# Second pair of blocks: the output gate's columns move into the joint Strassen projection, and the value projection moves from the front of attention into the filler

## The chip, the cores and the metric

The kernel runs on one core of a Trainium2 chip. TensorE multiplies (it writes PSUM only), VectorE, ScalarE and GpSimd (POOL) do the rest, SyncE and the queues of ScalarE and GpSimd issue DMAs. The metric is the device time of one execution, in microseconds (us), as the median of several runs; lower is better.

## The reference

One layer of a hybrid decoder on 2048 prompt positions and 32 sample positions (8 sequences of 4), model width 1024, in float32:

```
h = rmsnorm(x, n1);  z = h @ w_in          # 1024 x 4864
hq, hf, hi, hg, sq, sk, sv, ga, gb = split(z)   # 512 512 512 512 512 128 128 1024 1024
f = lb + (1 - lb) * sigmoid(hf)
o = hgrn_recurrence(hq, log f, 1 - f, hi)  # 4 heads of 128; hi are the values
y_a = (rmsnorm(o) * silu(hg)) @ w_up_a     # hg is the output gate
q, k, v = rotary(sq), rotary(sk), sv       # 8 query heads, 2 key/value heads of 64
y_b = sliding_window_attention(q, k, v, window 128, sinks) @ w_up_b
x = x + (sigmoid(ga) * y_a + sigmoid(gb) * y_b) @ w_o
x = x + square(relu(rmsnorm(x, n2) @ w_ff1)) @ w_ff2;  y = rmsnorm(x, nf)
```

The sample positions attend to a cache of 128 keys and start from a given recurrent state.

## The kernel before, in words

**Precision.** Every large product is made of three matmuls: each operand is split into a high part (a cast on ScalarE) and a low part (a subtraction on VectorE), and high x high, high x low and low x high are summed in PSUM. `unit_rows` (through `unit`, L138, and `split_out`, L257 and L258) loads a block of weights by SyncE's queue and splits it; a block takes three of twelve weight tiles (raw, high, low) of tag "w", and raw is free after the split. So 1024 rows by 128 columns are 24 matmuls per run of up to 512 tokens.

**Blocks and pairs.** The prompt is cut into four blocks of 512 tokens; the last one also carries the 32 sample tokens (544 tokens, run as two segments of 288 and 256). Blocks 0 and 1 are the first pair, blocks 2 and 3 the second. The loop `for bi in range(nblk)` does projections, attention, recurrence, the two merge gates and the output projection of a block. After it come the two feed-forward layers by pairs, with Strassen's scheme (seven products for eight).

**The second pair's joint projection.** With the flag `zs` (second pair) the even block first projects its own attention columns (`colN512(C_SQ ...)`, `colN(C_SQ + 512 ...)`) and sends q, k, v to DRAM (`zqk`). Then it runs one Strassen stage (`strassen_T`) over both blocks' 1056 tokens, cut into four quarters of 528 tokens by the two halves of the model width, for NZ = 20 column tiles: the recurrence's query (HH = 4 tiles) and the merge gates gb and ga (8 each). Column tiles go by twos (`Wpair`), tokens by two chunks of 264 (`chunks_of`), so there are 10 x 2 units. A `Unit` makes seven products (`prod`, L264 to L266) of 12 matmuls; VectorE adds the partial results in PSUM (L329, L342, L359, L372), ScalarE copies (L327). `z_fin` finishes a quarter: it writes tanh(x/2) for the merge gates (L861) or plain values for the query to the DRAM tensor `zd`, from which both blocks of the pair load later (`kmaj(zd[sb], ...)`).

**Front of attention.** In block 2, q, k, v come back from DRAM (L921) into a buffer that the stage's operand A22 occupied, then the recurrence's query is loaded into `qW` (L922), and `colN512(C_HI ...)` projects the values `vN` (L191 to L193, 96 matmuls). In block 3 the attention columns are projected directly (L892, L896), and the value projection (120 matmuls: four prompt tiles and one of 32 sample rows) runs between the steps of the sample's attention: `smp_scores`, `smp_turn` and `smp_values` hang on it as hooks (`smp_at`).

**Attention.** `tc.manual_schedule` keeps TensorE's instructions of this part in program order; elsewhere the framework's scheduler places every engine's instructions, and each engine then runs its own list in order. A tile c of 128 tokens has four steps: `swa_turn` T (rotation on POOL, L933 to L936, then transposes of q and k, L939, L942), `swa_scores` S (L1061, then softmax on VectorE and ScalarE), `swa_probs` P (transposes, L1094, masked products L1097 and L1099 on VectorE) and `swa_values` V (L1108). Between them `fill(n)` issues n x segments matmuls of the filler, a list of generators (`fills`): the forget gate, four heads of `col_steps(C_HF, ...)` (L684, finished by `ev_f`, L703 to L705), and then head 0 of the output gate, whose result is held in PSUM (`hg_held`). The order and the n are written by hand:

```
for f, c in ((T_, 0), (fill, 6), (S_, 0), (T_, 1), (fill, 12), (S_, 1), (T_, 2), (fill, 24), (P_, 0), (fill, 16), (V_, 0), (S_, 2), (T_, 3), (fill, 10), (P_, 1),
             (fill, 10), (V_, 1), (S_, 3), (fill, 10), (P_, 2), (fill, 8), (V_, 2), (fill, 16), (P_, 3), (fill, 8), (V_, 3)):
```

That is 120 steps (120 matmuls in block 2, 240 in block 3).

**Recurrence.** `hgrn_levels` runs seven levels (1 to 64) for two groups of 256 tokens, and two for the sample, as generators that take turns. A level is small matmuls (`lv`, L771), multiplications on VectorE (L776, L777, L779) and copies of results (L785, L788, L795). Level 0 is the only one that reads the decay `fW`; afterwards the output gate is written over it. So `ev_g` (L718 to L720: tanh and copy on ScalarE, multiplication on VectorE) may write head 0 only after round 1, and heads 1 to 3 are projected (`colT(C_HG, ...)`, L165 to L167) at rounds 3, 4 and 6 (`hg_at`). At rounds 3 and 5 the gb gates are loaded into `pb` (L1147). Then come `lx` (L805), the output o (L1193), the key transposes, the state update u, and `hgrn_tail`, which multiplies the normed output by the gate in `fW`. `split_out` splits it for the product with w_up_a.

**Merge gates.** `gate(C_GB, ...)` multiplies attention's output by w_up_b (`ybb`), whose weights `ub` are loaded ahead (r_ubb), and then `gate(C_GA, ...)` the recurrence's output by w_up_a.

Of the kernel before, what the change touches and what calls it, by code (L numbers as in the profile page):

```python
# [16 lines left out]
P = 128  # L17
# [21 lines left out]
def F(ap):  # L39
    return ap.bitcast(F32)  # L40
# [3 lines left out]
def tile_hybrid_step(  # L44
# [381 lines left out]
    NZ = HH + 2 * KD  # L426
# [205 lines left out]
    for bi in range(nblk):  # L632
# [193 lines left out]
        if zs and not odd:  # L826
# [29 lines left out]
            with tc.tile_pool(name=f"zp{sb}", bufs=1, reuse_waits="tile") as zp:  # L856
                def z_fin(u, blk, x, ps=None):
                    o, nh = int(blk[1]) - 1, int(blk[2]) - 1
                    zi = 2 * u.n + nh
                    if zi >= HH:  # L860
                        nc.scalar.activation(x, x if ps is None else ps, AF.Tanh, scale=0.5)  # L861
# [6 lines left out]
                def z_src(n, kh):  # L868
                    zi = 2 * n
                    c0 = C_HQ + zi * P if zi < HH else (C_GB + (zi - HH) * P if zi < HH + KD else C_GA + (zi - HH - KD) * P)  # L870
# [16 lines left out]
        if smp and zs:  # L887
            nc.gpsimd.dma_start(qS, zd[sb][0:HH * P, z0:z0 + NS].rearrange("(h p) t -> p h t", p=P))
# [5 lines left out]
        def ev_skv(ps, kind, c, nr):  # L894
            ti = c if kind == "p" else ncb
            nc.scalar.activation(qkv[0:nr, ti, 512:768], ps, AF.Copy, scale=1.0 if bi else rs0[:, 0, c:c + 1])  # L896

# [21 lines left out]
        else:  # L919
            for c in range(ncb):  # L920
                nc.gpsimd.dma_start(qkv[:, c, :], zqk[sb][c * P:(c + 1) * P, :])  # L921
            nc.gpsimd.dma_start(qW, kmaj(zd[sb], 0, HH, z0 + ns, bt))  # L922
            colN512(C_HI, f"hi{B}", ev_v)
# [188 lines left out]
        fills = [col_steps(C_HF, h, f"hf{B}{h}", ev_f) for h in range(HH)] + [col_steps(C_HG, 0, f"hg{B}0", None, hg_held)]  # L1112

        def fill(n):
            while n and fills:
                if next(fills[0], fills) is fills:
                    fills.pop(0)
                else:
                    n -= 1

        T_, S_, P_, V_ = swa_turn, swa_scores, swa_probs, swa_values
        for f, c in ((T_, 0), (fill, 6), (S_, 0), (T_, 1), (fill, 12), (S_, 1), (T_, 2), (fill, 24), (P_, 0), (fill, 16), (V_, 0), (S_, 2), (T_, 3), (fill, 10), (P_, 1),
# [627 lines left out]
```

## Time and profile before

| | us |
|---|---|
| median of 3 runs | 2817.21 (2811.98 to 2823.4) |
| span of the profiled execution | 2810.0 |
| joint Strassen stage of the second pair | 758 to 965 |
| block 2: attention from its first turned query / first gate-b matmul | 986.6 / 1072.9 |
| block 3: end of its key/value projection / first turned prompt query / first gate-b matmul | 1236.1 / 1272.9 / 1366.2 |

The profile is one execution. A row of a group gives the line of the code, the engine, what is written from what, and the count, then the busy time and the mean of one. In the view by stage each engine's busy time stands beside its number of instructions, and PEclk is the share of full clock that TensorE was granted. [...] Rows of the timeline give start and duration. A DMA's row on its issuing queue is the issue, not the transfer.

### The profile page before, as it was taken

Reading aid. Unit: us, or ns where it says so; the run is one execution under the profiler, and the core shown is the slowest. Engines: PE = TensorE matmul, PEld = TensorE weight load, DVE = VectorE, ACT = ScalarE, POOL = GpSimd, SP = SyncE. Lnnn points to the kernel's source line nnn. Section 1 sums busy time; section 2 is a strip of 40 time slices with the busy share of each in tenths; the row PEclk is TensorE's granted clock in tenths of the full one; section 3 lists DMA queues with packets and bytes.
Section 4 is the critical chain, followed back from the end, with each engine's and each line's share of the span. In section 5 each row is a group of like instructions: output and inputs, shape, how many; then the busy total and the mean of one; then the engine's idle time right before and its main releaser. Section 6 shows DMA issues by size and latency. Waiting matters only on the chain.

```text
span 2810.0 us, 50089 instructions
## 1 busy us (share of the span) xinstructions
PE 2730.1 (97%) x20053; PEld 2403.9 (86%) x20053; DVE 1791.2 (64%) x2905; ACT 1110.0 (40%) x2070; POOL 490.9 (17%) x782
## 2 busy tenths in 40 slices
PE   8999999999999999899999999999999999999998
PEld 7778888788899977677898888878888999999998
DVE  5675746746774385637667777765567777654556
ACT  4542445423344353335334333434344233343332
POOL 1100211002300102320231221220012343320001
PEclk9999999999999999999999999999999999999999
DMA  5237662377743424652365544796566444485553
GB/s 190 75 103 237 208 198 76 97 242 256 251 126 115 144 76 149 219 160 67 105 210 184 181 145 150 265 317 222 190 200 215 147 161 135 155 291 184 189 187 119
DMA packets 344481, 487.60 MB, mean 174 GB/s; under 512 B 23432, under 2 KB 220824, under 8 KB 344248
## 3 DMA queue, kind: packets, MB, share of 16 engines
q1 hardware_dynamic: 289112, 329.10, 37.5%
q0 software_dynamic: 42880, 140.22, 13.8%
q10 hardware_dynamic: 12256, 15.08, 1.5%
q8 instruction: 157, 2.57, 0.4%
q14 instruction: 76, 0.62, 0.1%
HBM read 353.64 MB, written 130.68 MB: 172 GB/s over the span
## 4 chain that ended last, share of the span: by engine, by line
PE 78%; DMA 6%; DVE 6%; issue 5%; ACT 2%; POOL 2%; SPq 0%; POOLq 0%; DVEq 0%; ACTq 0%
PE f L1581 6%; PE f L1582 6%; PE f L1580 6%; PE fB_f L264 4%; PE fB_f L266 3%; PE fB_f L265 3%; PE fD_f L264 2%; PE fD_f L266 2%; PE fD_f L265 2%; PE ps_hfb L684 2%; PE fB_z L264 1%; PE fB_z L266 1%; PE fB_z L265 1%; PE wob L1390 1%; PE gab L166 1%
## 5 line engine op out<-in xcount | busy, mean ns | idle before, releaser
L1582 PE MATMUL f<-f2S,lw2T 128*128 128x264 f32 (+1 forms) x576 | 184.4, 320 | 2.0 <-DVE lw2T L152 2.0
L1580 PE MATMUL f<-f2S,hw2T 128*128 128x264 f32 (+1 forms) x576 | 184.5, 320 | 1.6 <-ACT hw2T L151 1.6
L1581 PE MATMUL f<-f2S,hw2T 128*128 128x264 f32 (+1 forms) x576 | 184.0, 319 | 0.0
L264 PE MATMUL fB_f<-S,w1T_f 128*128 128x264 f32 (+1 forms) x384 | 123.2, 322 | 3.1 <-ACT c_f L327 2.2
L152 DVE TENSOR_TENSOR lw2T<-lw2T,hw2T 128x1024 fp32r<-128x1024 f32 x64 | 78.2, 1224 | 69.7 <-ACT hw2T L151 68.8
L265 PE MATMUL fB_f<-S,w1T_f 128*128 128x264 f32 (+1 forms) x384 | 122.5, 319 | 0.0
L1580 PE MATMUL f<-f2A,h_w2B 128*128 128x264 f32 (+1 forms) x384 | 122.4, 319 | 0.0
L1581 PE MATMUL f<-f2A,h_w2B 128*128 128x264 f32 (+1 forms) x384 | 122.3, 319 | 0.0
L1582 PE MATMUL f<-f2A,l_w2B 128*128 128x264 f32 (+1 forms) x384 | 122.3, 318 | 0.0
L266 PE MATMUL fB_f<-S,w1T_f 128*128 128x264 f32 (+1 forms) x384 | 122.0, 320 | 0.0
L151 ACT CAST hw2T<-lw2T 128x1024 fp32r<-128x1024 f32 x64 | 67.2, 1051 | 137.2 <-DMA lw2T<-w_T 137.2
L1582 PEld LDWEIGHTS f<-f2S,lw2T 128*128 128x128 f32 x576 | 108.4, 188 | 10.4 <-DVE lw2T L152 2.9
L1580 PEld LDWEIGHTS f<-f2S,hw2T 128*128 128x128 f32 x576 | 108.8, 189 | 9.9 <-ACT hw2T L151 2.4
L1388 PE MATMUL wob<-m_b,h_wob 128*128 128x512 f32 (+2 forms) x320 | 113.1, 353 | 3.2 <-ACT h_wob L257 3.2
L1390 PE MATMUL wob<-m_b,l_wob 128*128 128x512 f32 (+2 forms) x320 | 112.4, 353 | 3.0 <-DVE l_wob L258 2.8
L1581 PEld LDWEIGHTS f<-f2S,hw2T 128*128 128x128 f32 x576 | 108.8, 189 | 7.6
L1389 PE MATMUL wob<-m_b,h_wob 128*128 128x512 f32 (+2 forms) x320 | 112.5, 352 | 0.0
L152 DVE TENSOR_TENSOR f2S<-f2S 128x1024 fp32r<-128x1024 f32 (+1 forms) x64 | 78.9, 1240 | 41.3 <-ACT f2S L151 40.9
L257 ACT CAST w1T_f<-w1r_f 128x512 fp32r<-128x512 f32 x128 | 77.1, 619 | 69.7 <-DVE w1r_f L300 29.7
L258 DVE TENSOR_TENSOR w1T_f<-w1r_f,w1T_f 128x512 fp32r<-128x512 f32 x128 | 87.4, 688 | 26.0 <-ACT w1T_f L257 25.7
L1507 POOL DMA_DIRECT2D u_A<-c_f x106 | 57.4, 541 | 236.1 <-DVE c_f L1491 225.1
L1507 POOL DMA_DIRECT2D u_S<-s_f x144 | 77.7, 541 | 109.0 <-DVE s_f L1502 92.4
(845 smaller groups left out, 9256.8 us busy)
## 6 DMA issues: line engine op xcount, KB each, us to landing
w1r_f<-w_ff SPq DMA_DIRECT2D x64, 512.0 KB
lw2T<-w_T SPq DMA_DIRECT2D x64, 512.0 KB
rw2B<-w_ff SPq DMA_DIRECT2D x48, 512.0 KB
f2S<-u_S SPq DMA_DIRECT2D x32, 528.0 KB
ws<-w_ff SPq DMA_DIRECT2D x32, 512.0 KB
r_wob<-w_o SPq DMA_DIRECT2D x32, 512.0 KB
f2S<-u_S SPq DMA_DIRECT2D x32, 512.0 KB
u_S<-s_f POOLq DMA_DIRECT2D x96, 132.0 KB, 2.3
```

The costliest lines, as they stand in the source:

```text
L152: pin(nc.vector.tensor_tensor(lo, F(lo), F(hi), ALU.subtract), on)
L258: pin(nc.vector.tensor_tensor(dl, src, F(dh), ALU.subtract), on)
L264: nc.tensor.matmul(ps, wh, ah, start=(first and k == 0), stop=False, skip_group_check=not first)
L265: nc.tensor.matmul(ps, wh, al, start=False, stop=False, skip_group_check=not first)
L266: nc.tensor.matmul(ps, wl, ah, start=False, stop=(last and k == 3), skip_group_check=not first)
L1388: nc.tensor.matmul(p, wh, ah, start=(k == 0), stop=False)
L1389: nc.tensor.matmul(p, wh, al, start=False, stop=False)
L1390: nc.tensor.matmul(p, wl, ah, start=False, stop=(k == KD - 1))
L1507: nc.gpsimd.dma_start(us[o][u.n // 4][u.n % 4 * P:(u.n % 4 + 1) * P, u.t0:u.t0 + u.ln], y_)
L1580: nc.tensor.matmul(ps, wh, ah, start=first, stop=False, skip_group_check=cont)
L1581: nc.tensor.matmul(ps, wh, al, start=False, stop=False, skip_group_check=cont)
L1582: nc.tensor.matmul(ps, wl, ah, start=False, stop=lastk, skip_group_check=cont)
```

## The change

Only the second pair changes.

- The output gate's four column tiles join the Strassen stage behind the query's: NZ goes from 20 to 24, 12 column pairs and 24 units. `z_fin` writes (1 + tanh(x/2)) x for them: tanh on ScalarE (into `carry` where x itself is not in PSUM), scalar_tensor_tensor on VectorE, the store on POOL's queue.
- The gate is no longer projected in the recurrence. `z_rows` loads it from DRAM into `fW` (and `fS`) at round 1 by POOL's queue. The norm weight, which `ev_g` multiplied in, is applied where the output is split.
- The value projection no longer stands in front of attention. It becomes a generator, `row_steps`, last in the filler: two token tiles first, then one at a time, with all four weight blocks kept.
- What the hand-written order does not use is issued by `fill(10000)` behind the levels in the program (the second pair only).
- The order of block 2 begins with 16 fill steps ahead of T_0 and has 112 in all; the order of block 3 takes in the sample's attention, also with 112 steps, where a step of the value projection counts two.
- Both blocks' query loads (`z_q`) come at one place, behind the load of q, k, v.

```diff
-    NZ = HH + 2 * KD
+    ZG, ZB, ZA = HH, 2 * HH, 2 * HH + KD
+    NZ = 2 * HH + 2 * KD
...
+        def row_steps(c0, name, fn):
+
+            us = []
+            for grp in [tiles[0:2]] + [[t] for t in tiles[2:]]:
+                ps = [mm_ps(f"ps_{name}_{t[3]}") for t in grp]
+                for i in range(KD // 2):
+                    if len(us) <= i:
+                        us.append(unit_rows(w_in, 2 * i, 2, c0, 512, f"{name}{i}"))
+                    uh, ul = us[i]
+                    for p, (kind, r0, nr, c) in zip(ps, grp):
+                        for kk in range(2):
+                            k = 2 * i + kk
+                            lh, ll = (x[:, r0:r0 + nr] for x in h_acts[k])
+                            for m, (a, w) in enumerate(((lh, uh), (lh, ul), (ll, uh))):
+                                nc.tensor.matmul(p[0:nr], a, w[:, kk, :], start=(k == 0 and m == 0), stop=(k == KD - 1 and m == 2))
+                                if k == KD - 1 and m == 2:
+                                    fn(p[0:nr], kind, c, nr)
+                                yield len(segs)
...
-                    if zi >= HH:
-                        nc.scalar.activation(x, x if ps is None else ps, AF.Tanh, scale=0.5)
-                    elif ps is not None:
-                        nc.scalar.copy(x, ps)
-                    q = nc.scalar if zi >= HH else nc.gpsimd
+                    src = x if ps is None else ps
+                    if zi < ZG:
+                        if ps is not None:
+                            nc.scalar.copy(x, ps)
+                    else:
+                        tg = carry[:, u.t0:u.t0 + u.ln] if ps is None and zi < ZB else x
+                        nc.scalar.activation(tg, src, AF.Tanh, scale=0.5)
+                        if zi < ZB:
+                            nc.vector.scalar_tensor_tensor(x, tg, 1.0, src, ALU.add, ALU.mult)
+                    q = nc.scalar if zi >= ZB else nc.gpsimd
...
-            nc.gpsimd.dma_start(qW, kmaj(zd[sb], 0, HH, z0 + ns, bt))
-            colN512(C_HI, f"hi{B}", ev_v)
+        if zs:
+            z_q()
...
-        if zs and odd:
-            nc.gpsimd.dma_start(qW, kmaj(zd[sb], 0, HH, z0 + ns, bt))
-            smp_at = {0: lambda: [smp_scores(kv) for kv in range(NKV)], 2: lambda: [smp_turn(kv) for kv in range(NKV)], 3: smp_values} if smp else {}
-            colN512(C_HI, f"hi{B}", ev_v, lambda i, ul: smp_at[i]() if i in smp_at else None)
...
-        fills = [col_steps(C_HF, h, f"hf{B}{h}", ev_f) for h in range(HH)] + [col_steps(C_HG, 0, f"hg{B}0", None, hg_held)]
+        fills = [col_steps(C_HF, h, f"hf{B}{h}", ev_f) for h in range(HH)]
+        fills += [row_steps(C_HI, f"hi{B}", ev_v)] if zs else [col_steps(C_HG, 0, f"hg{B}0", None, hg_held)]
...
+        elif not odd:
+            seq = ((fill, 16), (T_, 0), (fill, 6), (S_, 0), (T_, 1), (fill, 10), (S_, 1), (T_, 2), (fill, 20), (P_, 0), (fill, 10), (V_, 0), (S_, 2), (T_, 3), (fill, 8), (P_, 1),
+                   (fill, 8), (V_, 1), (S_, 3), (fill, 8), (P_, 2), (fill, 8), (V_, 2), (fill, 10), (P_, 3), (fill, 8), (V_, 3))
+        else:
+            seq = ((fill, 10), (q_scores, 0), (fill, 8), (T_, 0), (fill, 4), (S_, 0), (T_, 1), (q_turn, 0), (fill, 8), (S_, 1), (T_, 2), (q_values, 0), (fill, 18), (P_, 0), (fill, 10), (V_, 0),
+                   (S_, 2), (T_, 3), (fill, 8), (P_, 1), (fill, 8), (V_, 1), (S_, 3), (fill, 8), (P_, 2), (fill, 8), (V_, 2), (fill, 12), (P_, 3), (fill, 10), (V_, 3))
...
+                if rnd == 1:
+                    z_rows(fW, ZG, ns, bt)
+                    if smp:
+                        z_rows(fS, ZG, 0, NS)
...
+        fill(10000)
...
+                if zs:
+                    nc.scalar.activation(oa[:, 0, h, t0:t0 + n], gx[:, h, 0:n], AF.Copy, scale=hn5[:, h:h + 1])
+                    nc.vector.scalar_tensor_tensor(oa[:, 1, h, t0:t0 + n], gx[:, h, 0:n], hn5[:, h:h + 1], F(oa[:, 0, h, t0:t0 + n]), ALU.mult, ALU.subtract)
```

More of the change, by code (lines that the diff above doesn't have):

```diff
@@ L1117, in fill, with q_scores @@
                     fills.pop(0)
                 else:
[L1119 to L1123 removed]
+                    n -= m or 1
+        def q_scores(_):
+            for kv in range(NKV):
+                smp_scores(kv)
@@ L1124, in tile_hybrid_step @@
+        for f, c in seq:
             f(c * len(segs) if f is fill else c)
-        fill(1000)
+        if not zs:
+            fill(10000)
         pe_order.__exit__(None, None, None)
@@ L1155, in tile_hybrid_step @@
             rnd += 1
+        fill(10000)
         def hgrn_out(ops, nr, name):
```

39 lines of the change are left out of this document (26 added, 13 removed).

## The prediction

> **What bounds the kernel now.** I read the page first, for the engine that sets the end.
>
> ```profile
> PE 2730.1 (97%) x20053; PEld 2403.9 (86%) x20053; DVE 1791.2 (64%) x2905; ACT 1110.0 (40%) x2070; POOL 490.9 (17%) x782
> ...
> PE 78%; DMA 6%; DVE 6%; issue 5%; ACT 2%; POOL 2%; SPq 0%; POOLq 0%; DVEq 0%; ACTq 0%
> ```
>
> TensorE is busy 97% of the span and 78% of the chain that ended last. A change pays here by taking matmuls away or by filling the few places where TensorE stands still. The second view is the busy time by stage. I cut it at the second pair's joint projection, then for block 2 at the first turned query (T_0), at the first recurrence matmuls and at the first gate-b matmul; the last three rows cut block 3 likewise, from the end of its key/value projection.
>
> ```profile
> core 0: us, PE busy (x) PEld busy (x) DVE busy (x) ACT busy (x) POOL busy (x), PEclk, DMA share, GB/s
> 758.00:965.00 207.00, 206.86 (x1685) 205.06 (x1684) 112.09 (x200) 91.62 (x193) 11.68 (x21) 1.00 0.42 133
> 965.00:986.60 21.60, 21.60 (x95) 17.46 (x94) 4.24 (x4) 6.12 (x8) 10.82 (x20) 1.00 0.59 195
> 986.60:1026.40 39.80, 39.80 (x288) 30.55 (x286) 30.84 (x63) 24.74 (x87) 1.28 (x4) 1.00 0.20 54
> 1026.40:1072.90 46.50, 40.65 (x889) 29.85 (x888) 34.74 (x77) 17.83 (x43) 4.78 (x6) 0.96 0.41 117
> 1236.00:1272.90 36.90, 36.61 (x212) 28.38 (x210) 10.41 (x22) 13.50 (x30) 2.79 (x5) 1.00 0.41 116
> 1272.90:1327.50 54.60, 52.82 (x471) 45.72 (x470) 41.63 (x98) 31.09 (x115) 2.47 (x4) 1.00 0.20 51
> 1327.50:1366.20 38.70, 32.27 (x920) 30.24 (x918) 29.27 (x75) 14.80 (x39) 8.71 (x10) 0.91 0.43 123
> ```
>
> The joint projection is solid TensorE work. The value projection in front of attention (row two, and most of row five) is solid too, with VectorE nearly idle beside it. The recurrences (rows four and seven) are where TensorE stands: 5.85 us and 6.43 us, and their clocks of 0.96 and 0.91 lose up to 4% of 46.5 us (1.9) and 9% of 38.7 us (3.5) more. So the old idle time that a better filler could take is at most 17.7 us.
>
> **Matmuls that come and go.** For the direct gate projection I read starts in the timeline of TensorE: 24 matmuls of 512 columns in block 2, then 24 of 288 and 24 of 256 in block 3.
>
> ```profile
> 1050.76 0.50 PE L165 MATMUL ps_hgb<-hT,h_hgb 128*128 128x512 f32 x1
> ...
> 1056.54 0.34 PE L771 MATMUL lv_b2g<-W_b 128*32 128x16 f32 x19
> ...
> 1347.87 0.40 PE L165 MATMUL ps_hgb<-hT_b,h_hgb 128*128 128x288 f32 x1
> ...
> 1351.17 0.28 PE L165 MATMUL ps_hgb<-hT_b,h_hgb 128*128 128x256 f32 x1
> ...
> 1354.11 0.49 PE L771 MATMUL lv_b3g<-W_b 128*32 128x16 f32 x35
> ```
>
> From start to start one costs 5.78/24 = 0.241 us at 512 columns, 3.30/24 = 0.138 at 288 and 2.94/24 = 0.123 at 256. Four heads of 24 go away: 96 x 0.241 = 23.1 us in block 2 and 96 x (0.138 + 0.123) = 25.0 us in block 3. The Strassen stage ran 20 units (10 column pairs, two token chunks), 1685 matmuls in 207.0 us, 0.1229 us each. Two more pairs are 4 units of 84: 336 x 0.1229 = 41.3 us. Matmuls alone: 41.3 - 48.1 = **-6.8 us**. The seven-for-eight trade of Strassen is mostly eaten by 264-column matmuls that cost more per column.
>
> [...]
>
> The value projection keeps its matmuls (96 in block 2, 120 in block 3). Only their place changes.
>
> **Strassen stage, other engines.** VectorE's 112.09 us over 20 units is 5.6 us per 10.3 us unit; a gate unit adds four scalar_tensor_tensor and ScalarE four tanh. The nearest groups of that stage:
>
> ```profile
> L359 DVE TENSOR_TENSOR c_z<-fD_z,c_z 128x264 f32<-128x264 f32 x20 | 8.6, 430 | 19.8 <-ACT c_z L327 19.7
> L861 ACT ACTIVATE c_z<-c_z 128x264 f32<-128x264 f32 x43 | 18.2, 424 | 30.1 <-DVE c_z L359 12.4 <-DVE c_z L372 9.3 <-DVE c_z L329 4.2
> ```
>
> Four times 0.43 makes 7.3 us of VectorE per unit, under TensorE's 10.3. What is new is a wait: VectorE's multiply waits for ScalarE's tanh, and behind it stand the PSUM additions that free banks for TensorE. One such wait is about a tanh long, 0.42 us, and there are 16. If none shows it is 0, if half show 3 us. I take **+1**, since TensorE lost only 0.14 us in the whole stage. The gate stores go out on POOL's queue, idle here (11.68 of 207 us). The reload of the gates waits on that queue until level 0 of the recurrence has read the decay it overwrites; behind it stand the gate-b loads, which are first read at the first gate-b product, and the gates' own first reader is the first output tile. The rest of the recurrence covers both, so nothing is booked; without that cover it would be one load, about the 6 us that the q, k, v load below takes to its first use.
>
> **Front of attention, block 2.** The value projection covered the return of q, k, v from DRAM and the rotation on POOL:
>
> ```profile
> 964.04 2.12 POOL L921 DMA_DIRECT2D qkv_b<-zqk  x4 [2.87 <-PE fB_z L266]
> 970.14 1.25 POOL L933 TENSOR_TENSOR r_b2c<-qkv_b,rot 128x80 f32<-128x80 f32 x1 [3.97 <-ACT h_hfb L257]
> 971.35 0.35 POOL L934 TENSOR_TENSOR r_b2c<-qkv_b,rot 128x80 f32<-128x80 f32 x1
> 971.64 1.06 POOL L967 MEMSET qbd<- 128x1152 f32 x1
> ...
> 973.27 0.53 POOL L936 TENSOR_TENSOR qkv_b<-qkv_b,r_b2c 128x160 f32<-128x160 f32 x1
> ```
>
> The load is issued at 964.04, because its slot is freed by the last Strassen unit, and the first rotated tile is there at 973.80, 8.8 us after that stage ends at 965.05. TensorE's order is written by hand, so T_0 waits for it and everything behind T_0 too. The new cover is 16 forget-gate matmuls, 16 x 0.241 = 3.9 us. TensorE stands 4.9 us. After the last idle stretch of that length the granted clock fell:
>
> ```profile
> 1061.00:1071.00 10.00, 6.92 (x81) 5.17 (x81) 7.16 (x16) 5.36 (x14) 0.00 (x0) 0.83 0.05 16
> ```
>
> 17% of 10 us is 1.7 us more. I take **+6.6**. The unknown is the 6.1 us from issue to first use, which other loads shared; I allow half of it, 3.1 us, either way. Upper bound 9.7. Lower bound +1: 4.9 less 3.1 and less the MEMSET's 1.06 is 0.8, too short to move the clock.
>
> The first POOL operation took 1.25 us and its twin 0.35, beside a VectorE subtraction:
>
> ```profile
> 969.95 1.23 DVE L258 TENSOR_TENSOR l_hfb<-r_hfb,h_hfb 128x1024 fp32r<-128x1024 f32 x1 [4.26 <-PE ps_hib L192]
> ```
>
> This speaks against the change: the rotation is now on the path while weights are split beside it. [...]
>
> **Thinner fill in attention.** From T_0 on block 2 had 120 fill matmuls and now has 96; block 3 had 240 short ones, now 192 short and 16 long, two steps counted for each long one. Between the transposes of probabilities and the value product (P to V) the fill must cover VectorE:
>
> ```profile
> 1003.08 0.48 PE L684 MATMUL ps_hfb<-hT,h_hfb 128*128 128x512 f32 x1
> ...
> 1006.15 1.28 DVE L1099 TENSOR_TENSOR pc_b2c<-pT_b2c,pc_b2c 128x512 f32<-128x512 f32 x2
> ```
>
> The transposes end at 1003.08, the products are there at 1007.43: 4.35 us. The fill there goes from 16 to 10, 2.4 us, so 1.9 us open. The three later tiles go from 10, 8, 8 to 8 each and I give them 0.5 us each: 3.5 us per block, **+7** for both. Bounds 3 and 12.
>
> In block 3 the sample's softmax now has 24 short fills and one tile's scores with two turns to cover it, instead of 60 long matmuls:
>
> ```profile
> 1236.87 1.09 PE L964 MATMUL kcT<-ident,kc 128*128 128x128 f32 x8 [0.29 <-ACT SV_b L940]
> ...
> 1244.82 2.16 PE L987 MATMUL sps<-kcT,qbd 64*128 64x128 f32 x18
> ...
> 1248.38 0.30 PE L988 MATMUL sps<-kt_smp,qs 64*128 64x32 f32 x2
> ...
> 1259.74 0.30 DVE L1005 TENSOR_SCALAR ss<-ss,sms 128x160 f32<-128x160 f32 x1
> ...
> 1272.86 0.65 PE L939 MATMUL qT_b3c<-ident,qkv_b 128*128 128x128 f32 x4
> ...
> 1282.81 0.66 PE L939 MATMUL qT_b3c<-ident,qkv_b 128*128 128x128 f32 x4
> ```
>
> From the last score at 1248.38 to the weights at 1260.04 it took 11.7 us, but it had time. From T_0 to T_2 are 9.95 us with 36 fills (36 x 0.13 = 4.7), so one tile's scores with two turns take about 3.0, and the new cover is 24 x 0.13 + 3.0 = 6.1 us. I take **+1**, bounds 0 and 5.6.
>
> **Recurrence.** What stood idle in block 2 was the gate-b weights, in block 3 the gate held in PSUM, which may not overwrite the decay before level 0 has read it:
>
> ```profile
> ACT h_ubb L257 <- DMA r_ubb<-w_up_b: 8.9, 1, 8.9
> DVE l_ubb L258 <- ACT h_ubb L257: 6.0, 1, 6.0
> ...
> ACT W_b L719 <- DVE W_b L777: 4.4, 1, 4.4
> ```
>
> In block 2 a weight cast blocked ScalarE's and VectorE's queues, and with them the levels, so TensorE ran dry. Value rows have neither constraint: they write their own tile, leave PSUM with one copy, and can be placed from the first level on. Left for the recurrence are 80 of 96 in block 2 (72 gate matmuls before) and 104 of 120 long ones in block 3 (144 short before). I take 8 of block 3's 9.9 us back, and 4 of block 2's 7.8, because value weights hold eight of the twelve weight tiles meanwhile and a late weight can stall the same queues. **-12**, bounds -17.7 and -4.
>
> **The sum.** -6.8 + 1 + 6.6 + 7 + 1 - 12 = -3.2 us. On the profiled span of 2810.0 this is 2806.8. The median of the runs, 2817.21, lies 7.2 above that span, so I expect 2814.0. All low ends make -6.8 + 0 + 1 + 3 + 0 - 17.7 = -20.5 (2796.7); all high ends -6.8 + 3 + 9.7 + 12 + 5.6 - 4 = +19.5 (2836.7).
>
> **Rivals.** *Faster: the filler takes all old idle time.* For it: both causes named above go away with the gate. Then T_0 at 1, thin fill at 7, sample at 1, no tanh waits and the full 17.7: -15.5 us, 2801.7. Against it: the twelve weight tiles. Chance 0.26.
>
> *Slower: attention becomes bound by the chain through VectorE.* T_0 to gate b would last as long as now (86.3 us in block 2, 93.3 in block 3) whatever is filled. Block 2 then gains only its earlier T_0, 21.6 - 8.8 - 1.7 = 11.1 us. In block 3 only the transposes (2.0 us from 1236.0), the scores (1244.82 to 1248.68, 3.9) and 36 short fills (4.7) stand before T_0: 10.6 us instead of 36.9, 26.3 gained, but the sample's 10.41 us of VectorE move into the stretch: 15.9. Together 27.0 against 41.3 + 1: +15.3 us, 2832.5. It decides if VectorE's load there, 10.41 + 41.63 + 29.27 = 81.3 us, cannot be packed into about 100 us. For it: 41.63 of 54.6 us now. Against: twelve gate multiplications leave VectorE. Chance 0.08.
>
> *The value rows do not fill.* They are written after the level loop; if the scheduler leaves them there, 184 x 0.241 = 44.3 us run behind the levels. With half of it uncovered: 41.3 + 1 - 11.1 - 26.3 + 22.2 = +27.1 us, 2844.3. Against it: the gate matmuls of now are cut into pieces of 24 and fewer between levels (the rows from 1050.76 to 1056.54 are one). Chance 0.04.
>
> **How the numbers follow.** The forecast, 2814.0, has 0.62. I use 0.5%, 14 us, as what a measurement of this kernel can tell from no change: below 2803 is faster, above 2831 slower. The first rival is faster (0.26); the second sits on the line and is halved; the third is slower: slower 0.08, same 0.66. The range 2797 to 2830 takes in the first rival and the low end, and leaves out the third and the worst corner.
>
> **What would show it.** Right: about 41 us more in the Strassen stage at 0.123 us a matmul; T_0 of block 2 some 9 us after it, with TensorE idle for about 5 us and one clock step; value matmuls between the levels; TensorE idle in both recurrences below 12.3 us. Wrong: value matmuls in a row behind the last level, waits of TensorE for VectorE of over 5 us per block in attention, or the Strassen stage longer by more than 44 us.

## The result: slower by 0.9%

The changed kernel takes 2841.98 us (median of 4 runs, 2837.70 to 2844.35); the kernel before, run beside it, 2815.32 us. The ratio is 1.0090 (95% interval 1.0073 to 1.0108), 26.7 us more. The forecast was 2814.0 us with a range of 2797 to 2830; the time lies above even the sum of all its high ends, 2836.7. The profiled execution has a span of 2842.4 us, 32.4 us over that of before.

First the page of the changed kernel: busy time by engine, and the chain that ended last.

```profile
PE 2740.9 (96%) x20101; PEld 2411.6 (85%) x20101; DVE 1799.6 (63%) x2931; ACT 1108.9 (39%) x2072; POOL 496.2 (17%) x801
...
PE 69%; issue 13%; DMA 7%; DVE 6%; ACT 3%; POOL 2%; SPq 0%; POOLq 0%; DVEq 0%; ACTq 0%
```

TensorE stands 101.5 us of this span and stood 79.9 us of the other. The shares of the chain must not be read as lost time: TensorE's fell from 78% to 69% and "issue" (the engine waited for nothing that the profile shows) rose from 5% to 13%, but a second profile of the kernel before (e5 below) has 70% and 13%. Where time is lost is seen by stage: the Strassen stage, then for block 2 and for block 3 four stretches: **front** (to T_0), **attention** (T_0 to the last V), **levels** (to the first output tile o) and **output** (to the first gate-a product).

```profile
core 0: us, PE busy (x) PEld busy (x) DVE busy (x) ACT busy (x) POOL busy (x), PEclk, DMA share, GB/s
758.70:1006.98 248.28, 247.84 (x2021) 245.90 (x2021) 136.73 (x250) 110.14 (x235) 20.33 (x37) 1.00 0.41 129
1006.98:1014.46 7.48, 3.17 (x16) 2.25 (x14) 0.43 (x1) 1.37 (x2) 3.75 (x8) 1.00 0.97 351
1014.46:1066.40 51.94, 47.80 (x416) 34.84 (x416) 38.74 (x81) 28.53 (x103) 8.18 (x18) 0.97 0.19 52
1066.40:1105.30 38.90, 35.03 (x871) 26.15 (x870) 23.94 (x56) 8.53 (x20) 3.64 (x5) 0.91 0.36 112
1105.30:1144.97 39.67, 37.13 (x225) 32.01 (x224) 24.32 (x47) 14.62 (x45) 10.02 (x16) 1.00 0.42 126
1269.10:1279.49 10.39, 10.10 (x87) 9.71 (x86) 2.41 (x6) 4.03 (x10) 2.79 (x5) 1.00 0.43 133
1279.49:1342.57 63.08, 55.29 (x426) 45.69 (x424) 43.75 (x110) 32.68 (x125) 2.47 (x4) 0.89 0.21 57
1342.57:1386.74 44.17, 41.32 (x1026) 30.33 (x1025) 26.73 (x66) 10.04 (x22) 6.46 (x12) 0.92 0.33 102
1386.74:1449.25 62.51, 57.41 (x418) 49.26 (x416) 37.84 (x72) 17.50 (x58) 9.04 (x14) 1.00 0.51 150
```

The kernel before, cut in the same way (block 2's attention, levels and output, then block 3's; the fronts are in the prediction):

```profile
986.63:1038.00 51.37, 51.23 (x413) 37.85 (x411) 42.14 (x84) 30.51 (x107) 3.13 (x6) 1.00 0.23 64
1038.00:1075.18 37.18, 31.47 (x833) 24.18 (x832) 25.72 (x60) 12.79 (x25) 2.93 (x4) 0.95 0.44 128
1075.18:1112.04 36.86, 36.42 (x282) 31.76 (x282) 21.94 (x48) 12.18 (x43) 10.08 (x16) 1.00 0.30 96
1272.86:1327.29 54.43, 52.65 (x472) 45.76 (x470) 41.63 (x98) 31.09 (x115) 2.47 (x4) 1.00 0.20 52
1327.29:1368.01 40.72, 34.20 (x990) 31.62 (x989) 31.08 (x78) 15.55 (x41) 8.71 (x10) 0.92 0.45 134
1368.01:1426.31 58.30, 57.21 (x475) 49.30 (x475) 35.46 (x73) 14.71 (x56) 9.12 (x14) 1.00 0.42 126
```

Read each row twice: span less PE busy is idle time, and (1 - PEclk) x span is what the clock took. The two kernels give (us; before is its first profile):

| stretch | before: span, idle + clock | after: span, idle + clock |
|---|---|---|
| Strassen | 207.0, 0.1 | 248.3, 0.4 |
| block 2 front / attention | 21.6, 0.0 / 51.4, 0.1 | 7.5, 4.3 / 51.9, 5.7 |
| block 2 levels / output | 37.2, 7.6 / 36.9, 0.4 | 38.9, 7.4 / 39.7, 2.5 |
| block 3 front / attention | 36.9, 0.3 / 54.4, 1.8 | 10.4, 0.3 / 63.1, 14.7 |
| block 3 levels / output | 40.7, 9.8 / 58.3, 1.1 | 44.2, 6.4 / 62.5, 5.1 |

The Strassen stage grew by 41.3 us as counted; block 2 shrank from 147.0 to 138.0 us and block 3 from 190.3 to 180.1 us. So the two blocks are 19.2 us shorter, though 48.1 us of gate matmuls left them. The lost time (idle and clock) of the two blocks rose from 21.1 to 46.4 us, 25.3 more: with the -6.8 us of the matmul trade that makes +18.5, and the stages together show +22.1; 3.6 us are not accounted for by this count. Of the other 10.3 us of the 32.4, 9.5 lie behind block 3's output projection, where the first profile of before was a short one (last section).

Three places stand out. At T_0 of block 2 the hand-written order waits for the rotation:

```profile
PE qT_b2c L969 <- POOL qkv_b L966: 4.3, 1, 4.3
```

In block 3's attention three steps wait for copies on ScalarE and products on VectorE, and behind the longest one TensorE, though busy all the time, runs at half clock for 10.2 us:

```profile
PE po_s L1052 <- ACT SV_b L970: 2.7, 1, 2.7
PE sp_b3c L1086 <- ACT kt_b3c L974: 2.0, 1, 2.0
PE po_b3c L1133 <- DVE pc_b3c L1124: 1.5, 2, 1.4
```

```profile
1297.70:1307.90 10.20, 10.20 (x62) 9.75 (x61) 3.62 (x12) 3.55 (x15) 0.00 (x0) 0.50 0.00 0
```

And the value rows stand in a row behind the last level, 9.1 us in block 2 (32 of the 80 left for the recurrence; shown are the first and the last, between lx and o) and 11.2 us in block 3 (48 of 104). The others did run beside the levels:

```profile
1095.71 0.56 PE L825 MATMUL lx_b2g<-W_b 128*32 128x1 f32 x46 [0.88 <-issue]
1096.21 0.68 PE L708 MATMUL ps_hib<-l_hib,hT 128*128 128x512 f32 x1
...
1105.06 0.39 PE L708 MATMUL ps_hib<-h_hib,hT 128*128 128x512 f32 x1
1105.30 0.38 PE L1246 MATMUL o_b2o<-SV_b,W_b 128*128 128x128 f32 x2
```

### The profile page after: what moved, and what is told of

It is laid out like the page before. It is cut to its first block, busy times and chain, and to the rows that moved or that the text cites. A ratio compares the mean times of both kernels' runs of the same rounds, so it can differ in the third digit from the quotient of the medians.

```text
span 2842.4 us, 50269 instructions
## 1 busy us (share of the span) xinstructions
PE 2740.9 (96%) x20101; PEld 2411.6 (85%) x20101; DVE 1799.6 (63%) x2931; ACT 1108.9 (39%) x2072; POOL 496.2 (17%) x801
## 3 DMA queue, kind: packets, MB, share of 16 engines
q1 hardware_dynamic: 282904, 327.01, 36.5%
q8 instruction: 158, 2.59, 0.4%
## 4 chain that ended last, share of the span: by engine, by line
PE 69%; issue 13%; DMA 7%; DVE 6%; ACT 3%; POOL 2%; SPq 0%; POOLq 0%; DVEq 0%; ACTq 0%
PE f L1638 6%; PE f L1639 6%; PE f L1637 6%; PE fB_f L264 4%; PE fB_f L266 4%; PE fB_f L265 3%; PE fD_f L264 2%; PE fD_f L266 2%; PE fD_f L265 2%; PE ps_hib L708 2%; PE wob L1447 1%; PE wob L1445 1%; PE wob L1446 1%; PE ps_hfb L685 1%; PE gab L167 1%
## 5 line engine op out<-in xcount | busy, mean ns | idle before, releaser
L1637 PEld LDWEIGHTS f<-f2S,hw2T 128*128 128x128 f32 x576 | 108.6, 189 | 10.4 <-ACT hw2T L151 2.9
```

Source lines behind the costliest of these rows:

```text
L1637: nc.tensor.matmul(ps, wh, ah, start=first, stop=False, skip_group_check=cont)
```

## The experiments

Theory A: the matmul trade is about nil and the loss is placement, work that no longer lies beside the levels. Theory B: it is the bare front and thin fill of attention. Further theories came up on the way. Ratios are to the kernel before on the same chip.

| kernel | ratio (95%) | block 2: front, attention, levels, output = sum | block 3 |
|---|---|---|---|
| before, first / second profile | 1 | 21.6, 51.4, 37.2, 36.9 = 147.0 / 149.1 | 36.9, 54.4, 40.7, 58.3 = 190.3 / 191.2 |
| after | 1.0090 (1.0073-1.0108) | 7.5, 51.9, 38.9, 39.7 = 138.0 | 10.4, 63.1, 44.2, 62.5 = 180.1 |
| e1 gates only | 1.0022 (1.0013-1.0031) | 21.6, 47.9, 28.3, 32.1 = 129.9 | 36.9, 50.4, 30.4, 56.0 = 173.7 |
| e2 values in levels | 1.0050 (1.0035-1.0065) | 7.6, 52.8, 33.6, 36.5 = 130.5 | 10.4, 62.8, 46.0, 60.6 = 179.8 |
| e3 front 36 | 1.0030 (1.0019-1.0041) | 9.1, 50.2, 31.4, 38.7 = 129.4 | 10.4, 62.8, 42.7, 60.9 = 176.8 |
| e4 thick attention | 1.0082 (1.0052-1.0112) | 9.2, 64.8, 29.9, 32.1 = 136.0 | 14.7, 79.5, 33.2, 56.1 = 183.5 |
| e6 half front | 1.0025 (1.0013-1.0038) | 10.9, 49.1, 28.5, 39.5 = 128.0 | 26.7, 56.6, 36.6, 57.2 = 177.2 |
| e7 block 3 front | 1.0013 (0.9998-1.0027) | 8.7, 50.2, 30.8, 38.2 = 127.9 | 36.9, 50.4, 28.0, 56.6 = 171.8 |
| e8 block 3 order | 1.0034 (1.0019-1.0048) | 8.7, 50.3, 29.9, 38.8 = 127.6 | 10.4, 73.5, 36.0, 59.4 = 179.3 |
| e9 after, late loads | 1.0090 (1.0075-1.0106) | 7.8, 53.5, 35.1, 47.2 = 143.6 | 10.4, 62.5, 42.4, 62.9 = 178.3 |
| e10 block 3 front, late loads | 1.0022 (1.0007-1.0037) | 9.0, 50.2, 28.1, 37.0 = 124.3 | 36.9, 52.0, 27.6, 60.6 = 177.0 |
| e11 before, late loads | 0.9978 (0.9963-0.9992) | 21.6, 51.2, 31.8, 38.3 = 142.9 | 36.9, 54.7, 40.0, 57.5 = 189.1 |
| e12 mended | 0.9996 (0.9985-1.0007) | 9.2, 50.2, 28.1, 35.5 = 123.0 | 36.9, 50.4, 28.5, 56.1 = 171.9 |

**e1: the Strassen half of the change alone.** The value projection goes back in front of attention, block 3's with the sample's hooks; the filler is the forget gate only, in both blocks in the order of block 2 without its first 16 steps.

```diff
+        if zs and not odd:
+            colN512(C_HI, f"hi{B}", ev_v)
...
-        fills += [row_steps(C_HI, f"hi{B}", ev_v)] if zs else [...]
+        fills += [] if zs else [...]
```

> The gate's columns come from the joint Strassen stage as in the change, but the value projection stands in front of attention as before, in both blocks, and the filler is the forget gate alone (96 steps from T_0 on). Theory A (the matmul trade is about nil, -6.8 us, and the loss is work that no longer lies beside the recurrence's levels): the levels are bare. In the changed kernel the stretch from the last V step to lx shrank by 9 us per block while 17 to 19 us of gate matmuls left it, so 8 to 10 us per block of cover are lost: -6.8 + 18 + a few us of thin fill = +11 to +15, 2826 to 2831 us. Rival B (all of the loss is the bare front of attention, T_0 and the sample's steps without cover): that front is covered again here, so 2808 to 2818 us, as before or a little faster.

Measured 2827.57 against 2821.21 us, +6.4 us: between the two, less than A's +11 to +15. So the Strassen half costs some 6 us and the move of the values the other 19 or so (0.68 points of ratio). A's mechanism is there. These are block 2's and block 3's levels:

```profile
1076.31:1104.58 28.27, 20.28 (x832) 15.98 (x830) 24.29 (x60) 6.57 (x16) 3.64 (x5) 0.88 0.47 152
1348.19:1378.54 30.35, 20.66 (x843) 18.78 (x842) 24.06 (x64) 6.59 (x16) 5.03 (x10) 0.66 0.49 162
```

With the gate's matmuls gone the levels shrink from 37.2 and 40.7 us only to 28.3 and 30.4, and lose 8.0 + 3.4 and 9.7 + 10.3 us to idle time and clock. By the prediction's prices the 72 and 144 gate matmuls that lay there cost 17.4 and 18.8 us, so about half of that time had been hidden. A's cost came out smaller, and one reason is in the trace: the scheduler found other filler, which the expectation had not counted, gate-b products.

```profile
L167 PE MATMUL ybb<-ob_b,l_ubb 128*128 128x512 f32 x8 | 3.4, 422 | 0.0
L166 PE MATMUL ybb<-ob_b,h_ubb 128*128 128x512 f32 x8 | 3.4, 420 | 0.0
L165 PE MATMUL ybb<-ob_b,h_ubb 128*128 128x512 f32 x8 | 3.2, 420 | 0.0
```

In block 2, 24 of them run ahead of the first output tile here, 4 in the kernel before, none in the changed kernel. There the value rows take their place, and the gate-b products are left for the output stretch, which is 32.1 us here and 39.7 us in the changed kernel.

**e2: the value rows inside the level loop.**

```diff
+                if rnd in range(1, 8):
+                    fill(len(segs) * (15 if odd else 12))
```

> The changed kernel with the value rows issued inside the level loop (12 steps after each level in block 2, 15 in block 3) in place of one call behind it. Theory A (the rows run behind the last level only because they are written there): the 32 and 48 matmuls in a row ahead of the first output tile become fewer than 10, and the idle time of TensorE between the last V step and lx (5.2 us and 2.9 us) and its clock loss (1.7 and 3.3 us) go: 8 to 13 us less, 2829 to 2834 us. Rival B (the loss is in attention): the rows move, the time stays within 3 us of 2842.

By the ratios the time falls by 11 us, within A's 8 to 13. A holds in block 2: levels and output 70.1 instead of 78.6 us, idle 2.1 instead of 6.4. In block 3 nothing is gained: the rows no longer stand behind the levels, but one stall of 4.7 us came in, and the stretch has a clock of 0.93 (changed kernel: 0.92).

```profile
PE lv_b3g L791 <- issue: 5.6, 2, 4.7
```

What it probably waited for is in the last section. Being written behind the loop is thus only part of the loss: even placed well, 80 rows (19.3 us at 0.241) make levels and output of block 2 9.7 us longer than in e1 (70.1 against 60.4), and 104 rows (25.1 us) those of block 3 20.2 us (106.6 against 86.4). Half of the rows' time is hidden in block 2, a fifth in block 3.

**e3: more cover ahead of T_0.**

```diff
-            seq = ((fill, 16), (T_, 0), ...
+            seq = ((fill, 36), (T_, 0), ...
```

> The changed kernel with 36 fill steps ahead of T_0 of block 2 in place of 16; the value rows start earlier for it, and 20 fewer run behind the levels. Both theories: TensorE's wait of 4.3 us for the rotation at T_0 goes. Theory A: 4 to 6 us less, 2836 to 2838 us. Theory B (the bare front is what costs): the wait and the clock step behind it go, and the later waits of block 2 shrink with them: 8 us or more less, 2834 us or under. If the wait only moves to the next step: 2842 us.

B's number, 8 us or more: block 2 is 8.6 us shorter. TensorE's idle time at T_0 is 1.3 instead of 4.3 us and attention keeps its clock (1.00 where the changed kernel has 0.97), so front and attention last no longer than in the changed kernel (59.3 against 59.4 us) with 20 steps (4.8 us) more in them. Those are missing behind it: levels and output take 70.0 instead of 78.6 us, so part of the gain is A's. By the ratios the time falls by 17 us; 3.4 of them are in block 3, which the edit does not touch, and the rest is not placed.

**e4: all value rows in attention.** Six fill steps more in each gap of block 2 and 36 ahead of T_0, eight or nine more in block 3.

> The changed kernel with thicker fill throughout attention: 36 steps ahead of T_0 in block 2, six more in every later gap (192 in all), nine more in every gap of block 3 (about 216), so that all value rows lie in attention and none beside or behind the levels. Theory B (attention is bound by latencies that thin fill leaves open): the idle time and clock loss of attention, about 8 us in block 2 and 14 in block 3, go, and the levels give back less than that: 2822 to 2832 us. Theory A (the loss is work missing beside the levels): attention gains, the levels are bare and lose 8 to 10 us per block against the kernel before: 2832 to 2842 us.

B fails here: the ratio is that of the changed kernel. Block 3's attention and levels:

```profile
1284.99:1364.46 79.47, 71.15 (x496) 55.61 (x494) 44.99 (x104) 35.13 (x124) 3.91 (x6) 0.96 0.18 47
1364.46:1397.66 33.20, 20.96 (x885) 19.00 (x884) 24.95 (x62) 8.58 (x18) 5.02 (x10) 0.69 0.57 176
```

Attention still has 8.3 us of idle time under eight or nine more steps in every gap, and the bare levels lose 12.2 + 10.3 us. Thick fill does not close those waits; it takes its matmuls from where they were worth something.

**e5: the kernel before, profiled again.** No edit.

> The kernel before, profiled once more, for one question only: the first feed-forward stage of the second pair lasts 342.3 us in the one profile of before and 346.8 to 351.1 us in the five profiles with the gate in the Strassen stage, though neither change nor experiments touch it. If that is the spread of one kernel's executions, this profile shows 345 us or more there; if the change causes it, it stays within 1.5 us of 342.3.

Span 2827.8 us, 17.8 over the first profile of the same code; the stage in question took 345.2 us, which speaks for spread. Block 2's levels took 39.4 instead of 37.2 us, block 3's 41.8 instead of 40.7. The first profile of before was a short execution; differences of 2 us in one stretch between two single profiles mean nothing.

**e6: half of the values in front, half in the levels**, cut by columns.

```diff
+        if zs and not odd:
+            colN(C_HI, f"hi{B}", ev_vh(0))
...
+        fills += [half_steps(C_HI + 256, f"hj{B}", ev_vh(256))] if zs else [...]
...
+                if rnd in range(1, 8):
+                    fill(18 if odd else 14)
```

> The gate from the Strassen stage; the value projection cut by columns: the first 256 columns of all token tiles in front of attention (11.8 us of matmuls in block 2, 14.8 us in block 3), the other 256 inside the level loop (14 steps of 0.123 us after each level in block 2, 18 in block 3); the filler of attention is the forget gate alone. Theory A (the loss is placement: the front needs some 9 us of cover, the levels some 12 to 15 us of it, and neither half of the change gives both): no wait at T_0, TensorE's idle time between the last V step and the first output tile under 4 us per block instead of 8.0 and 9.7 us in the first experiment; block 2 about 125 us and block 3 about 168 us, together -44 us against +41 us in the Strassen stage: 0 to 6 us under the kernel before. Rival C (VectorE's chain through the levels sets their length whatever is placed beside it): the levels grow by as much as is put there, block 2 stays at 129 us or more and block 3 at 173 us or more, 6 us over the kernel before.

Rival C's numbers nearly: block 3 stays at 177.2 us. Its front has 5.4 us of idle time of another kind: ScalarE's copy of a value tile stood behind a weight cast that waited 4.9 us for its weights. In block 2 idle time in the levels falls to 2.9 us as A has it, but the gate-b products are pushed out again (output 39.5 us). So the sum moves little: 128.0.

**e7: block 2 with e2's and e3's edits, block 3 with the values in front as in e1.**

> Block 2 with both mends (36 fill steps ahead of T_0, value rows inside the level loop), block 3 with the value projection in front and the sample's steps hanging on it as in the first experiment. If the two mends of block 2 work on different idle times (4.3 us at T_0 with its clock step, 5 us beside the levels), they add: block 2 about 126 us. Block 3 as in the first experiment, 173 to 174 us. In all 1 to 6 us over the kernel before. If the two mends take the same rows twice, block 2 stays at 129 to 131 us, and the time is 4 to 10 us over it.

The time is as expected, 1.0013 (3.7 us over), block 3 at 171.8 us. Block 2 comes to 127.9 us, between the two forecasts; the two mends together bring 10.1 us where alone they bring 7.5 and 8.6, so they share part of the same rows.

**e8: e2 and e3, and block 3's attention in another order**, the sample's transposes and value product one step later, 12 steps ahead of S_0.

> Both mends of block 2, and in block 3 value rows inside the level loop and another order of attention: 12 steps ahead of S_0 in place of 4, the sample's transposes and its value product one step later each (behind T_2 and P_0), 128 steps in place of 112. Theory: the waits for ScalarE's copies at S_0 (2.0 us), the sample's transposes (1 us) and its value product (2.8 us) close, and with them goes the stretch of half clock (10.2 us) that followed them in the changed kernel: T_0 to the last V of block 3 takes, against its 63 us, some 8 to 10 us less beside 4 us of rows more, 55 to 59 us. The time is then 0 to 8 us over the kernel before. If the waits only move to the next step, that stretch stays at 62 us or more and the time is 8 to 14 us over it.

The waits only moved, and grew:

```profile
PE pTs L1040 <- ACT SV_b L970: 4.0, 1, 4.0
PE po_s L1052 <- DVE pc_b3c L1124: 3.8, 1, 3.8
PE po_b3c L1133 <- DVE pc_b3c L1124: 2.0, 2, 1.3
```

The sample's steps on TensorE stand behind prompt tiles' copies and products on ScalarE and VectorE, in both orders. In front of attention, beside the value projection, they cost nothing: there block 3's front has 0.3 us of idle time (e1, e7).

**e9: the changed kernel with its gate loads made to wait for the last level.** The loads of gb and of the output gate leave rounds 1, 3 and 5:

```diff
+        if zs:
+            done = hres[-1][0][:, 0, 0:1]
+            for j in range(0, KD, 2):
+                nc.vector.tensor_copy(pb[:, j, 0:1], done)
+                nc.gpsimd.dma_start(pb[:, j:j + 2, :], kmaj(zd[sb], ZB + j, 2, z0, T))
+                if j == 0:
+                    nc.vector.tensor_copy(fW[:, 0, 0:1], done)
+                    z_rows(fW, ZG, ns, bt)
...
```

> The changed kernel with one edit: the loads of the gb gates (four of 544 KB or 512 KB) and of the output gate wait for the last level's product, so none of them runs beside the levels. Theory F (TensorE's instructions come in blocks of 16 KB, one per about 256 instructions or one level, and a block is late when gate loads fill the DMA engines; the traces show 3.6 to 3.7 us between blocks at the least, 5 to 7 us beside loads, and TensorE standing 2.1 to 4.9 us until some 2.5 us after a late block's start): the stalls of 2.1 us in block 2 and 2.5 us in block 3 that end with a late block go, with their stretches of half clock: 4 to 9 us less from the last V step to the first output tile in both blocks together, 2833 to 2838 us where the changed kernel has 2842. Rival (the loads are needed by then): the gate-b products wait for them behind the levels, and the time is 2842 us or more.

Both happened, and the time is the rival's: 1.0090, as for the changed kernel. Block 2's levels and output:

```profile
1069.52:1104.57 35.05, 32.62 (x870) 24.23 (x869) 24.12 (x57) 8.53 (x20) 3.67 (x5) 1.00 0.22 70
1104.57:1151.75 47.18, 39.58 (x225) 34.61 (x224) 24.32 (x47) 14.63 (x45) 10.02 (x16) 0.89 0.50 147
```

The levels are 3.9 us shorter (block 3's 1.7) and at full clock (1.00 in both blocks); block 2's output stretch, which now waits for the gates, is 7.5 us longer (block 3's 0.4).

**e10: e7 with the same late loads.**

> The kernel of the seventh experiment (block 2 mended, values in front in block 3) with the same late loads. Theory F: block 3's levels are bare there, their blocks of instructions come 4 to 6 us apart; without loads they come 3.7 us apart: 28.0 us from the last V step to the first output tile become 25 to 27 us, and the clock there rises from 0.70; 2 to 6 us less than the seventh experiment in all, at or a little under the kernel before. Rival (the gate-b products that lay between the levels now wait for their gates): what is gained there is lost behind it, and the time is that of the seventh experiment or up to 5 us more.

In block 2, where value rows lie beside the levels, it pays (127.9 to 124.3 us). In block 3 the bare levels stay at 27.6 us and a clock of 0.69, so the loads did not set their length: Theory F fails there, and the last section shows what TensorE waits for instead. The gates come late and block 3's output grows by 4.0 us. The time is the rival's, 1.0022.

**e11: the kernel before with late gb loads**, nothing of the change in it.

```diff
-            if zs and rnd in (3, 5):
-                for j in (2 * rnd - 6, 2 * rnd - 4):
...
+        if zs:
+            done = hres[-1][0][:, 0, 0:1]
+            for j in range(0, KD, 2):
...
```

> The kernel before with the same edit for its gb loads, nothing of the change in it. Theory F: the stall of 4.8 us (5.3 us in the second profile) in block 2's levels, which ends 3.2 us after a block of instructions that came 6.9 us behind the one ahead of it, with the DMA engines full, goes with its half clock, and in block 3 the stall of 2.3 us: 5 to 11 us less than the kernel before, a ratio of 0.996 to 0.998. Rival (that stall was the wait of ScalarE and VectorE for the gate-b weights, as the prediction read it): the time is that of the kernel before, within 3 us.

Faster than the kernel before, 0.9978 (0.9963 to 0.9992). The gain is in block 2's levels: 31.8 us at full clock (1.00), where the two profiles of before have 37.2 and 39.4 at 0.95 and 0.91. The number was forecast by Theory F, but its reason is not the one that the trace shows. TensorE's stall of 4.4 us in the first profile of before stands behind the weight cast, as the prediction had read it (the cast runs from 1059.58 to 1060.62, VectorE goes on at 1060.66, TensorE at 1064.08); here TensorE's idle time in the whole stretch is 1.6 us, where it was 5.7. With the gate loads behind the levels ScalarE's longest wait for these weights is 4.8 us, where the two profiles of before have 8.9 and 10.0:

```profile
ACT h_ubb L257 <- DMA r_ubb<-w_up_b: 7.2, 2, 4.8
```

**e12: what helped, together**: e7, with late gate loads in block 2 only.

> All that helped in one kernel: the gate from the Strassen stage; block 2 with 36 fill steps ahead of T_0, value rows inside the level loop and its gate loads behind the levels (124.3 us in the tenth experiment); block 3 with the values in front and the gate loads at their old rounds (171.8 us in the seventh). If the parts add, the stretch from the Strassen stage to the end of block 3's output projection is 248.3 + 124.3 + 124 + 171.8 + 72.4 = 740.8 us, where the two profiles of the kernel before have 740.7 and 743.7: the time is that of the kernel before within 4 us (ratio 0.9985 to 1.0015), and 3 to 8 us over the kernel before with late loads alone. If something of the change pays that the earlier runs hid, it is 5 us or more under the kernel before. If the matmul trade is worse than the -6.8 us counted, it is 4 us or more over it.

0.9996 (0.9985 to 1.0007). From the Strassen stage to block 3's last output projection 740.5 us, the 740.8 of the sum. The parts add, and with its losses mended the change still gains nothing. The late loads are in it too, and alone they bring 0.22% (e11): against e11 the same stretch of the profile is 4.8 us longer. e11 stays the fastest kernel of this study.

## Why the prediction was wrong, point by point

- **Matmuls, -6.8 us: right.** The Strassen stage took 41.3 us more, and e12 fits with it. The remark that 264-column matmuls eat up the trade is wrong by the prediction's own rows: 0.1229 us at 264 columns is 0.466 ns a column, 0.241 us at 512 is 0.471 (from start to start: in the changed kernel's rows a matmul of 264 columns takes 0.28 us and the next one starts after 0.12, so they overlap), and 41.3 against 48.1 us is 14% less, where seven for eight is 12.5%.
- **Strassen stage, other engines, +1: small, as held.** TensorE lost 0.44 us there, 0.14 before.
- **Front of block 2, +6.6: right.** 4.3 us of waiting and 1.6 us of clock loss in attention, 5.9. T_0 came 7.5 us after the stage; the row of 1.25 us for POOL, which the prediction held against the change, did not come back: the four operations took 0.35 to 0.52 us, and no subtraction of VectorE ran beside them (between 1007.6 and 1017 us it has no row). That the subtraction made the one row long is not shown by more than that row.
- **Thin fill and the sample, +7 and +1: too small.** Attention lost 5.6 us more in block 2 (1.6 of it the clock already counted at T_0) and 12.9 us more in block 3, 16.9 where 8 were booked (the bounds together reached 17.6). Block 3 is the miss: I priced the sample's steps by the cover of their softmax alone. What they waited for was the queue of ScalarE's and VectorE's work for the prompt tiles, and a half clock came behind it that no term had.
- **Recurrence, -12: the step that failed.** The levels' idle time and clock loss fell by 3.6 us (17.4 to 13.8), the output stretches' rose by 6.1 (1.5 to 7.6): +2.5 instead of -12, the one term outside its bounds. The prediction held that value rows can be placed from the first level on; they were written behind the loop, and 9.1 and 11.2 us of them ran there in a row, which the prediction had named as a sign of being wrong. e2 shows that this is worth 8.4 us in block 2's levels and output and nothing in block 3's. The rest, read from e1, is that the levels were not empty: the gate's matmuls had filled them before, and gate-b products do it when these are gone.
- **The rivals.** "The value rows do not fill" had the place right (20.3 us in a row behind the levels, 22.2 booked) and the time (2844.3) within 2.3 us, at a chance of 0.04. The closeness is partly luck: fronts and attention gave back 31.3 us where it booked 37.4, and levels and output grew by 12.2 us where it booked 22.2. "Attention becomes bound by the chain through VectorE" expected T_0 to gate b to last as before, 86.3 us in block 2 and 93.3 in block 3. It was 93.4 and 109.8, and from block 3's front to its last V step TensorE waited 6.5 us for ScalarE and 1.5 us for VectorE. "The filler takes all old idle time" was wrong.
- The argument against the third rival, that gate matmuls were cut into pieces between levels, did not carry over: those were written inside the loop.

## What to carry to other kernels

Before moving matmuls out of a stage that waits, ask what lay hidden there: removed work that was hidden gives nothing back, here 11 to 14 of 48 us (e1 against the two profiles of before). A filler has worth by where its instructions are written and by what it pushes out; cover at a wait that a hand-written order cannot avoid was worth no less than cover beside the levels (8.6 us at T_0 in e3 against 7.5 in e2's block 2; 8.3 us at the sample's steps in e7 against nothing in e2's block 3). And look at loads that start beside a stage full of small steps: a gate that is needed later can be loaded later (e11), as long as the next stage does not then wait for it (e9).

## What was not expected of the hardware, and what stays open

**Instructions come in blocks of 16 KB.** The page of the changed kernel lists two instruction queues. The larger one is taken here for TensorE's, which has 40202 of the 50269 instructions:

```profile
q8 instruction: 158, 2.59, 0.4%
```

158 blocks in 2.59 MB are 16 KB each; for 20101 matmuls and as many weight loads that makes 254 instructions a block, an estimate from this page, since no row names the engine. One level is 128 small matmuls, with their weight loads 256 instructions, issued in 1.25 us (1056.54 to 1057.79 in the kernel before). The starts of these blocks in the trace's DMA records, in block 3's levels:

```
e2   1349.41  1355.58  1359.60  1366.01   gate loads fill the DMA engines to 0.9 and more from 1353.3 to 1355.1; TensorE stands 1353.27 to 1358.00
e10  1355.68  1360.04  1363.51  1367.06   no gate loads; gaps of up to 1.4 us between levels
```

In the levels two starts lie 3.5 us apart at the least (3.47 here in e10, 3.48 in the changed kernel, 3.72 in the kernel before). In six stalls by "issue" TensorE went on 2.3 to 2.7 us after a block's start (e2: 1355.58 to 1358.00; the changed kernel: 1070.42 to 1072.76, 1075.34 to 1077.91, 1093.23 to 1095.71 and 1353.39 to 1356.11; the kernel before: 1333.61 to 1336.09). That it waited for the block is inferred from this; for a stall of 2.4 us in the kernel before, which ends at 1331.08, the last block's start ahead of it is at 1323.33. That a full DMA queue makes a block late is read from such coincidences only: e9's levels of block 3, without gate loads, have 3.1 us of idle time where the changed kernel has 2.9, and e11's gain had another cause. In block 3's bare levels late loads only change what TensorE waits for. Its largest waits there, with loads beside the levels (e7) and without (e10):

```profile
PE lv_b3g L791 <- DVE SV_b L808: 3.7, 4, 1.1
PE lv_b3g L791 <- issue: 2.4, 3, 1.4
...
PE lv_b3g L791 <- DVE SV_b L808: 4.4, 4, 1.4
PE lv_b3g L791 <- issue: 1.1, 3, 0.4
```

In all, waits by "issue" fall from 2.4 to 1.1 us, those for VectorE rise from 5.7 to 6.1, and the levels last 28.0 and 27.6 us. Without loads it is mostly VectorE (24.9 of 27.6 us busy) that TensorE waits for.

**The half clock outlasts the wait ahead of it.** The row of 10.20 us above is at 0.50 with TensorE busy throughout, the last 6.0 us of it with fill matmuls of 288 and 256 columns, and it follows a wait of 2.7 us. What 0.50 costs is seen in the kernel before: matmuls of 288 columns start 0.240 us apart at a clock of 0.50 (1337.20 to 1338.88) and 0.133 at 1.00 (1340.42 to 1341.35). Such stretches last 3.4 us (1014.46 to 1017.86, from the end of the 4.3 us at T_0), 6.8 us (1355.80 to 1362.60, from the end of a wait of 2.3 us) and 10.2 us in the changed kernel; e1's block 3 levels, with their gaps, have a mean clock of 0.66 over 30.35 us, as much as 20.6 us at half. So the length does not go by the wait alone: 10.2 us came after 2.7 us, and 3.4 us after 4.3. Why is open.

**The second pair's first feed-forward stage** took 342.3, 345.2 and 343.1 us in the three profiles with the direct gate, and 343.8 to 351.1 us in the eleven with the gate from the Strassen stage, though its code is the same: about 4 us more on average. But from block 3's last output projection to this stage the three take 625.2 to 630.2 us and the eleven 622.4 to 626.0, and from that projection to the end of the span the three take 1316.9 us on average and the eleven 1316.9 too. So nothing of the 26.7 us is shown to lie behind block 3; why the two stretches trade was not tried.
